# Delta-rule scan with two head groups in opposite row halves: 64x64 matmuls on alternating array quarters and a compact state

## The chip, the cores and the metric

The kernel runs on one core of a Trainium2 chip. The metric is the device time of one execution in microseconds. A core has a matmul engine (TensorE; PE in the profile, its weight loads PEld), a vector engine (VectorE; DVE), a scalar engine (ScalarE; ACT), a general engine (GpSimd; POOL) and a queue engine (SyncE; SP). Each runs its own instructions in their order and waits for the others by semaphores. TensorE multiplies a stationary operand (`lhsT`) by a moving one (`rhs`) and writes to PSUM, which has banks of 128 partitions by 512 float32.

## The reference

A decoder block with two token mixers on 1024 tokens of width 1024. Mixer A is a dilated window attention. Mixer B, which the change concerns, is a gated delta rule with 8 heads of 64 by 64, evaluated in 16 chunks of 64 tokens, one after the other:

```python
def step(state, inp):
    q_e, at, u_c, w_c, k_d, dec = inp
    v_new = u_c - jnp.einsum('bhck,bhkv->bhcv', w_c, state)
    o = jnp.einsum('bhck,bhkv->bhcv', q_e, state) + jnp.einsum('bhij,bhjv->bhiv', at, v_new)
    state = state * dec[..., None, None] + jnp.einsum('bhck,bhcv->bhkv', k_d, v_new)
    return state, o
```

Before the scan come projections, a causal convolution, norms and a triangular solve in each chunk; after it an RMS norm over each head's 64 outputs, a gate, an up-projection of both mixers, a sigmoid-gated merge, an output projection, a residual add and a last norm.

## The kernel before

All large products are float16 matmuls of a high and a low part: three matmuls of 128x512 for each eighth of the contraction (lines 150 to 152, helper `mm3_steps`). An object `Feed` holds the projections as units of 32 steps; a step (one tick) is those three matmuls. Code that has to wait for other engines calls `feed.tick(n)`, which puts n ticks of this filler on TensorE between its own matmuls. TensorE's order is thus the order in which the code is written; the other engines' instructions are ordered by the framework's scheduler, where `tc.high_priority()` moves some ahead.

The scan (lines 1164 to 1215) runs over 8 tiles `t` of 128 tokens and in each over two chunks `c2`, which lie in partitions 0 to 63 and 64 to 127. Everything of chunk `c2` lies in the row half `r`. In each chunk but the first:

- `pk` and `pq` (line 1180, PSUM tag S): four pairs of heads at a time, keys or queries (`kT`, `qT`: 128 partitions are two heads of 64) times the state `Sb`. `Sb` is 128 x 4 x 128: for each pair of heads a block-diagonal 128x128, half of it zeros, so that one matmul with contraction over 128 rows serves two heads. 8 matmuls with 128 moving columns.
- on VectorE `z = Rv - pk * bgk` (two operations on 64 partitions x 512), `oq = pq * eG`, `Sb *= dec`.
- `feed.tick(4)`, then `pvn` (line 1192, tag O): for each of 8 heads the solved triangle `U` times `z`, 64x64 matmuls, all in one row half and one column half of the array.
- `vn = pvn * rk`, `feed.tick(2)`, then `pS` (line 1200, tag G): 8 matmuls `kdec` times `vn` that read one row half and write the two column halves in turn; two additions into the diagonal blocks of `Sb`; `feed.tick(2)`.

After the two chunks of a tile `po` (line 1211, tag G) multiplies the masked scores `at` by `vn`: 16 matmuls of 64x64, eight in one quarter of the array, then eight in another. `ob = oq + po`, its square (ScalarE) and its sum follow. `PACE = (4, 2, 2)` holds the three tick counts. S and G have two banks each, O has one.

After the scan, `fac` is formed, `ob` is scaled for each tile (8 operations), `feed.tick(OB_LAG)` puts 12 ticks in between, and 8 groups of four 128x128 transposes (line 1231) bring `ob` into the layout of the gate `zs`, with two ticks between groups.

Ahead of the scan the step sizes `beta` and log decays `gg` are made from a small projection (lines 822 to 838), and one PSUM bank `pg` takes four small products (lines 845 to 855): the running sum of `gg` by `upto`, what is left by `later`, and the sums over a chunk.

A float32 matmul stands as one row in an order list and as two MATMUL instructions (two passes) in the trace; a float16 matmul and a transpose stand as one in both.

Of the kernel before, what the change touches and what calls it, by code (L numbers as in the profile page):

```python
# [56 lines left out]
def hybrid_block(ctx: ExitStack, tc: tile.TileContext, A):  # L57
# [718 lines left out]
    def conv_unit(hb, what, dst_of, then=None):  # L776

        def gen(w):
            for c in range(2):
                cidx = 4 * what + 2 * hb + c  # L780
                dst = dst_of(c)
                last = []
                for hf in range(2):
                    def take(p):
                        with tc.high_priority():
                            xc = pp_.tile([128, 515], F32, name="xc", tag="xc", bufs=2)
                            if hf == 0:
# [37 lines left out]
    beta = kp.tile([128, 8, 8], F32, name="beta")  # L825
    gg = kp.tile([128, 8, 8], F32, name="gg")
# [17 lines left out]
    ggf = gg.rearrange("p t h -> p (t h)")  # L844
    PE.matmul(pg[:, 0:64], lhsT=upto, rhs=ggf, start=True, stop=True, skip_group_check=True)
# [6 lines left out]
    for h2 in range(2):  # L852
        PE.matmul(pg[64 * h2:64 * h2 + 64, 128:192], lhsT=ones64,
                  rhs=gx.rearrange("p t c (q e) -> p (t c) q e", e=2)[:, :, :, h2],
                  start=False, stop=True, skip_group_check=True)
    SC.activation(eG.rearrange("p t h -> p (t h)"), pg[:, 0:64], AF.Exp)
# [18 lines left out]
    Sb = gp.tile([128, 4, 128], F32, name="Sb")  # L875
# [82 lines left out]
    def keys_side(hb):  # L958
# [202 lines left out]
    def pv(x):  # L1161
        return x.rearrange("p (h v) -> p h v", v=64)

    for t in range(8):
# [4 lines left out]
        oq = cp.tile([128, 8, 64], F32, name="oq", tag="oq", bufs=1)
        vn = cp.tile([128, 8, 64], F32, name="vn", tag="vn", bufs=2)  # L1170
        for c2 in range(2):
            ch = 2 * t + c2
            r = slice(64 * c2, 64 * c2 + 64)
            z = Rv[:, 0]
            if ch:
                z = cp.tile([128, 8, 64], F32, name="z", tag="z", bufs=1)
                pk, pq = [bank("S", 2), bank("S", 2)]
                for p, src in ((pk, kT), (pq, qT)):
                    for c in range(4):
                        PE.matmul(p[r, c * 128:c * 128 + 128], lhsT=src[c][:, ch], rhs=Sb[:, c],  # L1180
                                  start=(c == 0), stop=True, skip_group_check=True)
                with tc.high_priority():
                    TT(z[r], pv(pk[r]), bc(bgk[r, t], 64), ALU.mult)
                    TT(z[r], Rv[r, t], z[r], ALU.subtract)
                TT(oq[r], pv(pq[r]), bc(eG[r, t], 64), ALU.mult)
                TT(Sb, Sb, bc(dec[:, t, c2], 128), ALU.mult)
            else:
                GP.memset(oq[r], 0.0)
            feed.tick(PACE[0])
            pvn = bank("O", 1)  # L1190
            for h in range(8):
                PE.matmul(pvn[r, h * 64:h * 64 + 64], lhsT=U[h // 4][r, t, h % 2, (h % 4) // 2], rhs=z[r, h],  # L1192
                          start=(h == 0), stop=True, skip_group_check=True)
            with tc.high_priority():
                TT(vn[r], pv(pvn[r]), bc(rk[r, t], 64), ALU.mult)
            feed.tick(PACE[1])
            pS = bank("G", 2)
            for h in range(8):
                e = slice(64 * (h % 2), 64 * (h % 2) + 64)
                PE.matmul(pS[e, h // 2 * 64:h // 2 * 64 + 64], lhsT=kdec[r, h], rhs=vn[r, h],  # L1200
                          start=(h < 2), stop=True, skip_group_check=True)
            with tc.high_priority():
                for h2 in range(2):
                    e = slice(64 * h2, 64 * h2 + 64)
                    TT(Sb[e, :, e], Sb[e, :, e], pS[e, :256].rearrange("p (c v) -> p c v", v=64), ALU.add)
            feed.tick(PACE[2])
        po = bank("G", 2)
        for c2 in range(2):
            r = slice(64 * c2, 64 * c2 + 64)
            for h in range(8):  # L1210
                PE.matmul(po[r, h * 64:h * 64 + 64], lhsT=at[h // 4][r, t, h % 2, (h % 4) // 2], rhs=vn[r, h],  # L1211
                          start=(h == 0), stop=True, skip_group_check=True)
# [9 lines left out]
    TT(fac, fac, rq, ALU.mult)  # L1222
# [3 lines left out]
    for hf in range(2):  # L1226
        for ct in range(4):
            ts = slice(hf * 512, hf * 512 + 512)
            p = bank("G", 2)
            for t in range(4):  # L1230
                PE.transpose(p[:, t * 128:t * 128 + 128],
                             ob[:, 4 * hf + t, 2 * ct:2 * ct + 2].rearrange("p h v -> p (h v)"), ident)
            STT(zs[ct][:, ts], p, gnw, zs[ct][:, ts], ALU.mult, ALU.mult)
# [182 lines left out]
```

## Time and profile before

| | |
|---|---|
| time, three runs | 1176.77, 1179.36 (median), 1180.28 us |
| profiled execution | 1178.9 us, of which the span of the core is 1177.1 us |
| VectorE busy | 775.3 us (66%) |
| ScalarE busy | 490.6 us (42%) |
| DMA, mean | 98 GB/s |
| the scan, first `pvn` to first filler behind the last `po` | 804.3 to 959.5 us |

Times of instructions are in us from the start of the span. A row of the timeline has the start, the duration, the engine, the line, the operation, output and inputs, the size and how many instructions were merged into the row; in square brackets stands how long the engine was idle before, and what ended that. A busy time of TensorE is modelled: the matmuls are pipelined, so that from one row's start to the next row's start is the time that a burst took of the engine, and the printed duration is longer than that.

### The profile page before, as it was taken

What the parts mean: (1) busy time and instruction counts of PE and PEld (TensorE: products, weight loads), DVE (VectorE), ACT (ScalarE), POOL (GpSimd) and SP (SyncE); (2) the same over time, 40 slices, a digit from 0 to 9 for tenths busy, and PEclk for the clock granted to TensorE, in tenths of its full rate; (3) what the DMA queues carried; (4) which work ended last, traced back from release to release, by engine and by line L of the source; (5) the groups of instructions that cost most, each with busy time, mean ns of one, the idle gap of its engine ahead of it and who ended that gap; (6) DMA issues with size and microseconds to landing.
All of it is one profiled execution on the core that took longest, in us unless ns stands there. A gap on an engine that the chain in (4) does not pass through costs nothing.

```text
span 1177.1 us, 22738 instructions
## 1 busy us (share of the span) xinstructions
PE 1151.2 (98%) x9134; PEld 708.2 (60%) x9134; DVE 775.3 (66%) x1737; ACT 490.6 (42%) x1125; POOL 57.9 (5%) x103
## 2 busy tenths in 40 slices
PE   6999999999999999999999999999999999999997
PEld 6884765857758556756555444556666654444443
DVE  5776747568475489568859979846766663675233
ACT  6445746566465455456545233333221123331211
POOL 2110000000000000000000000000000000100000
PEclk9999999999999999999999999999999999999999
DMA  7154333423434323523114341421110116440232
GB/s 265 62 143 122 110 100 91 127 81 83 140 91 113 97 76 99 151 91 96 41 54 125 96 135 55 99 73 63 46 32 33 46 45 258 159 165 1 72 108 72
DMA packets 73050, 115.24 MB, mean 98 GB/s; under 512 B 30560, under 2 KB 41184, under 8 KB 72816
## 3 DMA queue, kind: packets, MB, share of 16 engines
q1 hardware_dynamic: 56064, 65.14, 19.0%
q0 software_dynamic: 12128, 44.11, 11.8%
q10 hardware_dynamic: 4752, 4.52, 1.1%
q8 instruction: 72, 1.18, 0.4%
q14 instruction: 34, 0.28, 0.1%
HBM read 73.70 MB, written 21.17 MB: 81 GB/s over the span
## 4 chain that ended last, share of the span: by engine, by line
PE 75%; DVE 12%; DMA 4%; SPq 3%; ACT 3%; issue 2%; ACTq 0%; DVEq 0%
PE ps_mm L150 19%; PE ps_mm L151 18%; PE ps_mm L152 18%; SPq L466 3%; PE ps_S L1180 2%; PE ps_G L607 2%; PE ps_O L1192 1%; DVE wlo L62 1%; PE ps_G L950 1%; PE ps_G L1211 1%; DVE rt L65 1%; PE ps_S L152 1%; PE ps_S L150 1%; PE ps_S L151 1%; DVE tl L65 1%
## 5 line engine op out<-in xcount | busy, mean ns | idle before, releaser
L150 PE MATMUL ps_mm<-h_hi,whi 128*128 128x512 f16 (+1 forms) x912 | 345.0, 378 | 0.1
L151 PE MATMUL ps_mm<-h_lo,whi 128*128 128x512 f16 (+1 forms) x912 | 343.9, 377 | 1.0 <-DVE h_lo L65 1.0
L152 PE MATMUL ps_mm<-h_hi,wlo 128*128 128x512 f16 (+1 forms) x912 | 343.9, 377 | 0.0
L152 PEld LDWEIGHTS <-wlo 128*128 128x128 f16 x1088 | 106.4, 98 | 122.8 <-issue 1.2
L150 PEld LDWEIGHTS <-whi 128*128 128x128 f16 x1088 | 106.2, 98 | 87.3 <-issue 2.6
L151 PEld LDWEIGHTS <-whi 128*128 128x128 f16 x1088 | 106.5, 98 | 79.8 <-issue 0.3
L597 ACT ACTIVATE sm<-sm,osb 128x128 f32<-128x128 f32 (+1 forms) x192 | 85.0, 443 | 93.2 <-DVE osb L593 92.6
L62 DVE SCALAR_TENSOR_TENSOR wlo<-wstage,whi 128x1024 f16<-128x1024 f32 x80 | 97.2, 1222 | 37.7 <-ACT whi L136 37.4
L150 PE MATMUL ps_mm<-whi,h_hi 128*128 128x256 f16 x384 | 105.1, 274 | 0.0
L151 PE MATMUL ps_mm<-wlo,h_hi 128*128 128x256 f16 x384 | 104.7, 273 | 0.1
L152 PE MATMUL ps_mm<-whi,h_lo 128*128 128x256 f16 x384 | 104.7, 273 | 0.0
L136 ACT ACTIVATE whi<-wstage 128x1024 f16<-128x1024 f32 x79 | 82.6, 1054 | 44.7 <-PE ps_mm L151 40.5
L593 DVE CUSTOM_DVE_ANT_0 sm<-ps_S,amask 128x128 f32<-128x128 f32 (+1 forms) x192 | 59.5, 348 | 30.8 <-PE ps_S L586 30.6
L65 DVE TENSOR_TENSOR tl<-ps_G,th 128x256 f16<-128x256 f32 (+1 forms) x96 | 52.2, 544 | 39.2 <-ACT th L612 38.8
L132 POOL DMA_DIRECT2D wstage<-in_w x68 | 35.9, 528 | 809.2 <-DVE wlo L62 615.2
L65 DVE TENSOR_TENSOR rt<-rx,tabs 128x512 f32<-128x512 f32 x96 | 65.0, 688 | 15.3 <-ACT rx L439 14.3
L62 DVE SCALAR_TENSOR_TENSOR ca<-xc,cw,ca 128x512 f32<-128x512 f32 x72 | 53.8, 747 | 2.2 <-ACT ca L793 1.6
L150 PE MATMUL ps_mm<-wo_hi,m_hi 128*128 128x512 f16 (+2 forms) x136 | 49.5, 366 | 0.0
L151 PE MATMUL ps_mm<-wo_lo,m_hi 128*128 128x512 f16 (+2 forms) x136 | 49.5, 366 | 0.0
L152 PE MATMUL ps_mm<-wo_hi,m_lo 128*128 128x512 f16 (+2 forms) x136 | 49.4, 366 | 0.0
L607 PE MATMUL ps_G<-cons,sm 128*128 128x128 f32 x280 | 46.4, 273 | 2.0 <-DVE tl L65 2.0
L151 PEld LDWEIGHTS <-h_hi 128*128 128x128 f16 x384 | 45.8, 119 | 1.3
(264 smaller groups left out, 1928.9 us busy)
## 6 DMA issues: line engine op xcount, KB each, us to landing
wstage<-in_w POOLq DMA_DIRECT2D x68, 512.0 KB, 4.6
og<-osb ACTq DMA_DIRECT2D x32, 132.0 KB, 2.1
og<-og SPq DMA_DIRECT2D x32, 132.0 KB, 2.2
gspa<-gst SPq DMA_DIRECT2D x16, 256.0 KB, 2.0
wstage<-in_w_up POOLq DMA_DIRECT2D x8, 512.0 KB, 4.7
sga<-gspa SPq DMA_DIRECT2D x8, 512.0 KB, 5.0
wstage<-in_w_out POOLq DMA_DIRECT2D x8, 512.0 KB, 4.2
xr<-in_x SPq DMA_DIRECT2D x8, 512.0 KB, 4.2
```

Of the source, the lines that this page charges most:

```text
L62: (eng or V).scalar_tensor_tensor(out, in0, scalar, in1, op0=op0, op1=op1)
L65: (eng or V).tensor_tensor(out, in0, in1, op)
L132: (eng or nc.gpsimd).dma_start(out=st, in_=src[:, 4 * c:4 * c + 4])
L136: SC.activation(hi[:, 4 * c:4 * c + 4], st, AF.Copy, scale=W_SCALE)
L150: PE.matmul(out, lhsT=wh(k), rhs=mh(k), start=first and i == 0, stop=False, skip_group_check=True)
L151: PE.matmul(out, lhsT=wh(k), rhs=ml(k), start=False, stop=False, skip_group_check=True)
L152: PE.matmul(out, lhsT=wl(k), rhs=mh(k), start=False, stop=last and i == len(ks) - 1, skip_group_check=True)
L466: nc.sync.dma_start(out=o, in_=pt[name][32 * hd:32 * hd + 32])
L593: V.tensor_tensor_reduce(P[:, u, :128 * nk], psc[:, u * 256:u * 256 + 128 * nk], mask, -cexp, -NEG, ALU.add, ALU.min, accum_out=osb[:, 256 ...
L597: SC.activation(P[:, u, :128 * nk], P[:, u, :128 * nk], AF.Exp, bias=osb[:, 256 + hd:257 + hd], scale=-1.0, accum_out=osb[:, 260 + hd:261 ...
L607: PE.transpose(pt[:, c:c + 128], P[:, u, i * 128:i * 128 + 128], ident)
L1180: PE.matmul(p[r, c * 128:c * 128 + 128], lhsT=src[c][:, ch], rhs=Sb[:, c], start=(c == 0), stop=True, skip_group_check=True)
```

## The change

Heads 0 to 3 (`hb = 0`) stay as they were. For heads 4 to 7 (`hb = 1`) the two chunks of every tile swap their row halves. A chunk's eight heads then fill both row halves: four heads in one, four in the other, side by side in 256 columns in place of 512.

- The state becomes compact: `Sb` is 128 x 4 x 64, without the zero blocks. `pk` and `pq` become 16 matmuls of 64x64 for each head alone, which go through the four quarters in turn and share two banks (`pkq`), one for each row half that is read.
- `pvn` and `po` alternate between heads of the two groups, so that neighbouring matmuls lie in opposite quarters. `pS` writes two banks, one for each group.
- VectorE's operations of the scan work on 128 partitions: `vn` and `Sb *= dec` on 256 elements, `z`'s product and `oq` in two parts of 128, the subtraction in two parts of 64 partitions x 256, the additions into `Sb` in two parts of 128.
- What is multiplied along with them is laid out again: `by_chunk` copies `eG`, `rk`, `bgk` and `rq` into `eGs`, `rks`, `bgks`, `rqs`. The convolution's last operation writes heads 4 to 7 in two parts with the chunks swapped. For `beta` and `gg` two matmuls with a shifted identity swap the halves of heads 4 to 7, and ScalarE copies the result back (line 872 after the change) ahead of the products with `upto` and `later`.
- The first chunk's `z` is copied from `Rv` by ScalarE.
- The transposes behind the scan are 8 of 64 rows for each group in place of 4 of 128, into two banks, and the gate's multiplication is two operations.

```diff
+    hi4 = bg[:, :, :, 4:8]
+    for b in range(2):
+        PE.matmul(pg[64 * b:64 * b + 64, 192:256], lhsT=ident[:, 64 - 64 * b:128 - 64 * b], rhs=hi4,
                   start=False, stop=True, skip_group_check=True)
+    SC.copy(hi4, pg[:, 192:256].rearrange("p (a t h) -> p a t h", a=2, t=8))
+    PE.matmul(pg[:, 0:64], lhsT=upto, rhs=ggf, start=False, stop=True, skip_group_check=True)
+    PE.matmul(pg[:, 64:128], lhsT=later, rhs=ggf, start=False, stop=True, skip_group_check=True)
     SC.activation(eG.rearrange("p t h -> p (t h)"), pg[:, 0:64], AF.Exp)
+    by_chunk(eGs, eG)
...
-    Sb = gp.tile([128, 4, 128], F32, name="Sb")
+    Sb = gp.tile([128, 4, 64], F32, name="Sb")
...
+    order = [(hb, j) for j in range(4) for hb in range(2)]
...
-                pk, pq = [bank("S", 2), bank("S", 2)]
-                for p, src in ((pk, kT), (pq, qT)):
-                    for c in range(4):
-                        PE.matmul(p[r, c * 128:c * 128 + 128], lhsT=src[c][:, ch], rhs=Sb[:, c],
-                                  start=(c == 0), stop=True, skip_group_check=True)
+                pkq = [bank("S", 2), bank("S", 2)]
+                for i, src in enumerate((kT, qT)):
+                    for j in range(2):
+                        for n, (e, hb) in enumerate(((0, 0), (1, 1), (0, 1), (1, 0))):
+                            b, c, o = c2 ^ hb, 2 * hb + j, (2 * i + j) * 64
+                            PE.matmul(pkq[e][rows(b), o:o + 64], lhsT=src[c][rows(e), 2 * t + b], rhs=Sb[rows(e), c],
+                                      start=(i == 0 and j == 0), stop=True, skip_group_check=True)
                 with tc.high_priority():
-                    TT(z[r], pv(pk[r]), bc(bgk[r, t], 64), ALU.mult)
-                    TT(z[r], Rv[r, t], z[r], ALU.subtract)
-                TT(oq[r], pv(pq[r]), bc(eG[r, t], 64), ALU.mult)
-                TT(Sb, Sb, bc(dec[:, t, c2], 128), ALU.mult)
+                    for e in range(2):
+                        TT(z[:, e::2], hv(pkq[e][:, :128]), bc(bv[:, e::2], 64), ALU.mult)
+                    for hb in range(2):
+                        r = rows(c2 ^ hb)
+                        TT(z[r], Rv[r, t, 4 * hb:4 * hb + 4], z[r], ALU.subtract)
+                for e in range(2):
+                    TT(ov[:, e::2], hv(pkq[e][:, 128:256]), bc(ev[:, e::2], 64), ALU.mult)
+                TT(Sb, Sb, bc(dec[:, t, c2], 64), ALU.mult)
...
             pvn = bank("O", 1)
-            for h in range(8):
-                PE.matmul(pvn[r, h * 64:h * 64 + 64], lhsT=U[h // 4][r, t, h % 2, (h % 4) // 2], rhs=z[r, h],
-                          start=(h == 0), stop=True, skip_group_check=True)
+            for n, (hb, j) in enumerate(order):
+                r = rows(c2 ^ hb)
+                PE.matmul(pvn[r, j * 64:j * 64 + 64], lhsT=U[hb][r, t, j % 2, j // 2], rhs=z[r, j],
+                          start=(n < 2), stop=True, skip_group_check=True)
...
-            pS = bank("G", 2)
+            pS = [bank("G", 2), bank("G", 2)]
+            for q in range(2):
+                for hb, e in ((0, 0), (1, 1), (0, 1), (1, 0)):
+                    r, c = rows(c2 ^ hb), 2 * hb + q
+                    PE.matmul(pS[hb][rows(e), q * 64:q * 64 + 64], lhsT=kdec[r, 2 * c + e], rhs=vn[r, c2, 2 * q + e],
+                              start=(q == 0), stop=True, skip_group_check=True)
...
         po = bank("G", 2)
         for c2 in range(2):
-            r = slice(64 * c2, 64 * c2 + 64)
-            for h in range(8):
-                PE.matmul(po[r, h * 64:h * 64 + 64], lhsT=at[h // 4][r, t, h % 2, (h % 4) // 2], rhs=vn[r, h],
-                          start=(h == 0), stop=True, skip_group_check=True)
+            for n, (hb, j) in enumerate(order):
+                r, o = rows(c2 ^ hb), (4 * c2 + j) * 64
+                PE.matmul(po[r, o:o + 64], lhsT=at[hb][r, t, j % 2, j // 2], rhs=vn[r, c2, j],
+                          start=(c2 == 0 and n < 2), stop=True, skip_group_check=True)
...
-            p = bank("G", 2)
+            ps2 = [bank("G", 2), bank("S", 2)]
+            hb, h0 = ct // 2, ct % 2 * 2
             for t in range(4):
-                PE.transpose(p[:, t * 128:t * 128 + 128],
-                             ob[:, 4 * hf + t, 2 * ct:2 * ct + 2].rearrange("p h v -> p (h v)"), ident)
-            STT(zs[ct][:, ts], p, gnw, zs[ct][:, ts], ALU.mult, ALU.mult)
+                for b in range(2):
+                    c2 = b ^ hb
+                    PE.transpose(ps2[b][:, 64 * t:64 * t + 64],
+                                 ob[rows(b), 4 * hf + t, 4 * c2 + h0:4 * c2 + h0 + 2].rearrange("p h v -> p (h v)"),
+                                 ident[rows(b), rows(b)])
```

How instructions stand now, at the places that the prediction speaks of. On TensorE, the products with the state in the second chunk of the scan (`ps_S` is the bank, `Sb` the state, `kT` and `qT` with a buffer number are the pairs of heads). Before:

```order
L1180 MATMUL ps_S<-Sb,kT_740 64x128
L1180 MATMUL ps_S<-Sb,kT_741 64x128
L1180 MATMUL ps_S<-Sb,kT_742 64x128
L1180 MATMUL ps_S<-Sb,kT_743 64x128
L1180 MATMUL ps_S<-Sb,qT_8020 64x128
L1180 MATMUL ps_S<-Sb,qT_8021 64x128
L1180 MATMUL ps_S<-Sb,qT_8022 64x128
L1180 MATMUL ps_S<-Sb,qT_8023 64x128
```

On TensorE, the same place after the change:

```order
L1212 MATMUL ps_S<-Sb,kT_740 64x64
L1212 MATMUL ps_S<-Sb,kT_742 64x64 x2
L1212 MATMUL ps_S<-Sb,kT_740 64x64
L1212 MATMUL ps_S<-Sb,kT_741 64x64
L1212 MATMUL ps_S<-Sb,kT_743 64x64 x2
L1212 MATMUL ps_S<-Sb,kT_741 64x64
L1212 MATMUL ps_S<-Sb,qT_8027 64x64
L1212 MATMUL ps_S<-Sb,qT_8029 64x64 x2
L1212 MATMUL ps_S<-Sb,qT_8027 64x64
L1212 MATMUL ps_S<-Sb,qT_8028 64x64
L1212 MATMUL ps_S<-Sb,qT_8030 64x64 x2
L1212 MATMUL ps_S<-Sb,qT_8028 64x64
```

Eight products of 64x128 became sixteen of 64x64, with heads of the two groups in turn.

On VectorE, the fifth chunk's start, where a weight split (`wlo`) and the gate's work (`zs`) stand ahead of the scan's own `z`. Before:

```order
L65 TENSOR_TENSOR Sb<-Sb,ps_G 64x4x64 x2
L62 SCALAR_TENSOR_TENSOR wlo<-wstage,whi 128x1024
L62 SCALAR_TENSOR_TENSOR zs<-zt,ps_mm 128x512
L65 TENSOR_TENSOR z<-ps_S,bgk 64x512
L62 SCALAR_TENSOR_TENSOR zs<-zs,oTa_5297 128x512
L65 TENSOR_TENSOR z<-Rv,z 64x512
L65 TENSOR_TENSOR Rv<-oq,ps_G 128x512
L65 TENSOR_TENSOR osa_10654<-zs,osa_10654 128x512
```

On VectorE, the same place after the change:

```order
L65 TENSOR_TENSOR Sb<-Sb,ps_G 128x128 x2
L62 SCALAR_TENSOR_TENSOR wlo<-wstage,whi 128x1024
L62 SCALAR_TENSOR_TENSOR zs<-zt,ps_mm 128x512
L65 TENSOR_TENSOR z<-ps_S,bgks 128x2x64 x2
L62 SCALAR_TENSOR_TENSOR zs<-zs,oTa_5297 128x512
L65 TENSOR_TENSOR z<-Rv,z 64x256 x2
L65 TENSOR_TENSOR Rv<-oq,ps_G 128x512
L65 TENSOR_TENSOR osa_10716<-zs,osa_10716 128x512
L65 TENSOR_TENSOR vn<-ps_O,rks 128x256
```

The scan's operations are smaller and more, and the filler's operations stand among them at the same places; `vn` now comes ahead of the sum over `oq` and of `Sb *= dec`.

On TensorE, the small products ahead of the scan (`gx`, `bg` are what is multiplied, `cons` holds the constant matrices), after the change:

```order
L152 MATMUL ps_mm<-h_hi,wlo 128x512
L864 MATMUL ps_G<-gx,ones_6948 64x64 x2
L870 MATMUL ps_G<-bg,cons 64x64 x2
L874 MATMUL ps_G<-bg,cons 128x64
L875 MATMUL ps_G<-bg,cons 128x64
L150 LDWEIGHTS whi
```

Before, the two 128x64 products (lines 845 and 846) stood first and read `gg` directly; now they stand behind the swap on L870 and ScalarE's copy, with no filler in between.

More of the change, by code (lines that the diff above doesn't have):

```diff
@@ L806, in conv_unit, with by_chunk @@
         feed.add(("gdn", hb, what), A["w"][gdn_unit(hb, what)], gen)
+    def by_chunk(dst, x, hbs=(0, 1)):
+        for hb in hbs:
+            for b in range(2):
+                r = slice(64 * b, 64 * b + 64)
+                V.tensor_copy(dst[r, :, b ^ hb], x[r, :, 4 * hb:4 * hb + 4])
     gate_unit(1, gate_spill)
@@ L824, in hybrid_block @@
     STT(ba, pv[:, :, 0:16], P_SCALE, ba, ALU.mult, ALU.add)
-    beta = kp.tile([128, 8, 8], F32, name="beta")
-    gg = kp.tile([128, 8, 8], F32, name="gg")
+    bg = kp.tile([128, 2, 8, 8], F32, name="bg")
+    beta, gg = bg[:, 0], bg[:, 1]
     tmpa = pp_.tile([128, 8, 8], F32, name="tmpa")
@@ L839, in hybrid_block @@
     eG = kp.tile([128, 8, 8], F32, name="eG")
+    eGs = kp.tile([128, 8, 2, 4], F32, name="eGs")
     eGl = kp.tile([128, 8, 8], F32, name="eGl")
@@ L854, in hybrid_block @@
                   rhs=gx.rearrange("p t c (q e) -> p (t c) q e", e=2)[:, :, :, h2],
+                  start=True, stop=True, skip_group_check=True)
+    hi4 = bg[:, :, :, 4:8]
+    for b in range(2):
+        PE.matmul(pg[64 * b:64 * b + 64, 192:256], lhsT=ident[:, 64 - 64 * b:128 - 64 * b], rhs=hi4,
                   start=False, stop=True, skip_group_check=True)
+    SC.copy(hi4, pg[:, 192:256].rearrange("p (a t h) -> p a t h", a=2, t=8))
+    ggf = gg.rearrange("p t h -> p (t h)")
+    PE.matmul(pg[:, 0:64], lhsT=upto, rhs=ggf, start=False, stop=True, skip_group_check=True)
+    PE.matmul(pg[:, 64:128], lhsT=later, rhs=ggf, start=False, stop=True, skip_group_check=True)
     SC.activation(eG.rearrange("p t h -> p (t h)"), pg[:, 0:64], AF.Exp)
+    by_chunk(eGs, eG)
     SC.activation(eGl.rearrange("p t h -> p (t h)"), pg[:, 64:128], AF.Exp)
@@ L882, in hybrid_block @@
     bgk = gp.tile([128, 8, 8], F32, name="bgk")
+    rks = gp.tile([128, 8, 2, 4], F32, name="rks")
+    rqs = gp.tile([128, 8, 2, 4], F32, name="rqs")
+    bgks = gp.tile([128, 8, 2, 4], F32, name="bgks")
     def rnorm(dst, ssum, post):
@@ L963, in keys_side @@
         TT(bgk[:, :, hsl], brk[:, :, hsl], eG[:, :, hsl], ALU.mult)
+        by_chunk(bgks, bgk, (hb,))
+        by_chunk(rks, rk, (hb,))
         pack = p2_.tile([128, 2, 8, 4], F32, name="pack", tag="pack", bufs=1)
@@ L1159, in hybrid_block, with hv, rows @@
     ob = Rv
-    def pv(x):
+    def hv(x):
         return x.rearrange("p (h v) -> p h v", v=64)
+    def rows(b):
+        return slice(64 * b, 64 * b + 64)
+    order = [(hb, j) for j in range(4) for hb in range(2)]
     for t in range(8):
@@ L1194, in hybrid_block @@
             with tc.high_priority():
-                TT(vn[r], pv(pvn[r]), bc(rk[r, t], 64), ALU.mult)
+                TT(vn[:, c2], hv(pvn[:, :256]), bc(rks[:, t, c2], 64), ALU.mult)
             feed.tick(PACE[1])
-            pS = bank("G", 2)
-            for h in range(8):
-                e = slice(64 * (h % 2), 64 * (h % 2) + 64)
-                PE.matmul(pS[e, h // 2 * 64:h // 2 * 64 + 64], lhsT=kdec[r, h], rhs=vn[r, h],
-                          start=(h < 2), stop=True, skip_group_check=True)
+            pS = [bank("G", 2), bank("G", 2)]
@@ L1202, in hybrid_block @@
+            for q in range(2):
[3 more added lines that the diff above has]
+                              start=(q == 0), stop=True, skip_group_check=True)
             with tc.high_priority():
-                for h2 in range(2):
-                    e = slice(64 * h2, 64 * h2 + 64)
-                    TT(Sb[e, :, e], Sb[e, :, e], pS[e, :256].rearrange("p (c v) -> p c v", v=64), ALU.add)
+                for hb in range(2):
+                    sv = Sb[:, 2 * hb:2 * hb + 2]
+                    TT(sv, sv, hv(pS[hb][:, :128]), ALU.add)
@@ L1221, in hybrid_block @@
     V.reciprocal(fac, fac)
-    TT(fac, fac, rq, ALU.mult)
+    TT(fac, fac, rqf, ALU.mult)
     for t in range(8):
```

40 lines of the change are left out of this document (25 added, 15 removed).

## The prediction

> **What bounds the kernel now.** I read the page first (busy shares, then the chain of work that ended last), then the busy time by stretches for the scan alone, then the timeline of one chunk in it.
>
> ```profile
> span 1177.1 us, 22738 instructions
> PE 1151.2 (98%) x9134; PEld 708.2 (60%) x9134; DVE 775.3 (66%) x1737; ACT 490.6 (42%) x1125; POOL 57.9 (5%) x103
> PE 75%; DVE 12%; DMA 4%; SPq 3%; ACT 3%; issue 2%; ACTq 0%; DVEq 0%
> ```
>
> TensorE is busy 98% of the span and holds 75% of the chain. An average proves nothing for the scan, so the stretch from its first to its last product comes next (columns: the stretch, its length, then busy time and instructions of PE, PEld, DVE, ACT, POOL, then the granted clock, the DMA share and GB/s).
>
> ```profile
> 804.28:959.48 155.20, 155.20 (x1382) 97.19 (x1381) 102.25 (x164) 28.70 (x42) 3.75 (x8) 1.00 0.12 38
> ```
>
> In 155.2 us TensorE has no gap that this view shows, at full clock; VectorE is at 102.25 / 155.20 = 66%. Busy is modelled, so the timeline has to confirm it:
>
> ```profile
> 826.42 0.38 PE L152 MATMUL ps_mm<-h_hi,wlo 128*128 128x512 f16 x1
> 826.73 0.68 PE L1200 MATMUL ps_G<-vn,kdec 64*64 64x64 f32 x16
> 827.34 0.39 PE L150 MATMUL ps_mm<-h_hi,whi 128*128 128x512 f16 x1
> ...
> 828.74 1.09 PE L1180 MATMUL ps_S<-Sb,kT 128*64 128x128 f32 x8
> ...
> 829.66 1.04 PE L1180 MATMUL ps_S<-Sb,qT 128*64 128x128 f32 x8
> 829.86 0.69 DVE L65 TENSOR_TENSOR z<-ps_S,bgk 64x512 f32<-64x512 f32 x1 [1.56 <-PE ps_S L1180]
> ...
> 830.63 0.39 PE L150 MATMUL ps_mm<-h_hi,whi 128*128 128x512 f16 x1
> ...
> 833.33 1.14 PE L1192 MATMUL ps_O<-z,MT 64*64 64x64 f32 x16
> 834.40 0.39 PE L150 MATMUL ps_mm<-h_hi,whi 128*128 128x512 f16 x1
> 834.50 0.69 DVE L65 TENSOR_TENSOR vn<-ps_O,rk 64x512 f32<-64x512 f32 x1 [1.06 <-PE ps_O L1192]
> ...
> 835.80 0.68 PE L1200 MATMUL ps_G<-vn,kdec 64*64 64x64 f32 x16
> ```
>
> Every burst follows the filler with the same step, 0.31 us from 826.42 to 826.73. VectorE waits for TensorE (`vn` 1.06 us), not the other way: `vn` ends at 834.50 + 0.69 = 835.19 and is needed at 835.80. So what the small matmuls take from one row's start to the next comes straight off the span: `pk` and `pq` 830.63 - 828.74 = 1.89, `pvn` 834.40 - 833.33 = 1.07, `pS` 827.34 - 826.73 = 0.61.
>
> **The bursts, one by one.** `pvn` and `pS` have eight 64x64 products each (16 instructions). `pvn`, always in one quarter, takes 1.07; `pS`, whose neighbours write different column halves, 0.61. I read this as neighbours in different quarters overlapping. The other rows:
>
> ```profile
> 837.81 1.90 PE L1211 MATMUL ps_G<-vn,E 64*64 64x64 f32 x32
> 839.64 0.54 PE L1180 MATMUL ps_S<-Sb,kT 128*64 128x128 f32 x3
> ...
> 619.17 1.15 PE L950 MATMUL ps_G<-kT 64*64 64x64 f32 x32
> 620.26 0.39 PE L150 MATMUL ps_mm<-h_hi,whi 128*128 128x512 f16 x1
> ...
> 782.12 0.44 PE L1027 MATMUL ps_S<-T1p,MT 32*32 32x32 f32 x16
> 782.49 0.39 PE L150 MATMUL ps_mm<-h_hi,whi 128*128 128x512 f16 x1
> ```
>
> `po` takes 1.83 for sixteen products. L950, sixteen 64x64 products with the column halves in turn, takes 1.09. Sixteen at 1.09 and eight at 0.61 make 0.48 for eight more, or 0.06 for one product, and 0.13 for a burst's entry and exit. In L1027 (32x32) neighbours differ in row half and column half and write one bank: sixteen instructions in 0.37. If its products were serial like `pvn`'s, with half the columns, they would take (1.07 - 0.13) / 2 + 0.13 = 0.60. So row halves overlap as well. What the trace does not have is a neighbour in the same columns and the other rows, which the new `pkq` and `pS` have at every second step. Bounds: such a step is free, as above, or serial, which costs (1.07 - 0.61) / 8 = 0.06 for each. I take free, because both kinds of half that the trace shows are.
>
> - `pkq`, sixteen products, 1.09 in place of 1.89: 0.80 x 15 chunks = 12.0.
> - `pvn` at 0.61 in place of 1.07: 0.46 x 16 = 7.4.
> - `po` at 1.09 in place of 1.83: 0.74 x 8 = 5.9.
> - `pS`: still eight products with neighbours in turn, 0.
> - Behind `po` the next `pkq` follows at once, now in the same 64x64 shape: one entry and exit less, 0.13 x 7 = 0.9.
>
> Together **26.2 us less**.
>
> **What comes back.** VectorE's sizes, by rows that group all of a kind in the scan and in the merge before it:
>
> ```profile
> L65 DVE TENSOR_TENSOR Sb<-Sb,ps_G 64x256 f32<-64x256 f32 x32 | 13.4, 418 | 12.9 <-PE ps_G L1200 12.4
> L65 DVE TENSOR_TENSOR z<-ps_S,bgk 64x512 f32<-64x512 f32 x15 | 10.3, 688 | 10.2 <-PE ps_S L1180 10.0
> ...
> L65 DVE TENSOR_TENSOR Y<-ps_S,brk 32x128 f32<-32x128 f32 x32 | 9.3, 290 | 8.7 <-PE ps_S L1027 8.0
> ```
>
> 512 elements take 0.69, 256 take 0.42, 128 take 0.29; a count of partitions does not show (rows of 64 and 128 partitions agree). `z` stays near 1.4 (2 x 0.29 + 2 x 0.42 for 2 x 0.69), `vn` falls to 0.42, the additions from 2 x 0.42 to 2 x 0.29. A chunk's scan work on VectorE falls from 3 x 0.69 + 0.69 + 0.69 + 0.84 = 4.3 to 4 x 0.29 + 2 x 0.42 + 0.42 + 0.42 + 0.58 = 3.4. So nothing on the path grows, and a chunk's ticks (0.22 x 24 matmuls) still cover it. The cover is thin where filler work stands ahead, as in the fifth chunk:
>
> ```profile
> 838.79 1.22 DVE L62 SCALAR_TENSOR_TENSOR wlo<-wstage,whi 128x1024 f16<-128x1024 f32 x1 [1.31 <-ACT whi L136]
> 840.05 0.69 DVE L62 SCALAR_TENSOR_TENSOR zs<-zt,ps_mm 128x512 f32<-128x512 f32 x1
> ```
>
> `wlo` comes from the filler's pace and keeps its distance to the start of `po` (837.81), so `zs` ends at 840.74 as before. Behind it stand two products (0.58), another `zs` (0.69) and two subtractions (0.84): 842.85. TensorE, with `po` and `pkq` in 1.09 + 0.96 and 12 filler matmuls in 833.33 - 830.63 = 2.70, is there at 842.56, against 844.2 before. Queued behind the waiting `pvn` is the filler itself, so the 0.3 is lost. The eight `wlo` of the scan come in pairs, so this comes four times: I take **1.0** for waits of the scan, between 0 and 8 (below).
>
> Ahead of the scan the swap adds a round trip:
>
> ```profile
> 501.09 0.42 DVE L849 TENSOR_SCALAR gx<-gg,cons 128x64 f32<-128x64 f32 x2
> ...
> 501.20 0.41 PE L845 MATMUL ps_G<-gg,cons 128*128 128x64 f32 x2
> ...
> 501.76 0.33 PE L853 MATMUL ps_G<-gx,ones 128*64 128x64 f32 x4
> ...
> 502.03 0.39 PE L150 MATMUL ps_mm<-h_hi,whi 128*128 128x512 f16 x1
> ...
> 502.14 0.22 ACT L856 ACTIVATE eG<-ps_G 128x64 f32<-128x64 f32 x1 [0.30 <-PE ps_G L853]
> ```
>
> TensorE now waits for `gx` (done at 501.51), does eight instructions of L853's kind (to about 502.2), ScalarE copies in 0.22, and L845's and L846's kind takes 501.76 - 501.20 = 0.56 behind it: filler at about 503.2 in place of 502.03, **1.15 more**, since nothing is put in between. ScalarE's table load, now behind the copy, delays only `eG`.
>
> The solve of the triangles is the next cover:
>
> ```profile
> 699.73 0.43 PE L1044 MATMUL ps_O<-MT,Y 32*32 32x32 f32 x14 [0.51 <-DMA MT<-u_d]
> ...
> 651.32 0.18 DVE L966 COPY pack<-rk 128x32 f32<-128x32 f32 x1
> 651.41 0.18 DVE L65 TENSOR_TENSOR stmp<-As,X 128x31 f32<-128x31 f32 x1
> ```
>
> TensorE already waits 0.51 for the solved blocks there, so VectorE's additions before it are not hidden: four small copies at 0.10 (the step from 651.32 to 651.41) and about three convolution outputs in two parts (2 x 0.42 - 0.69 = 0.15 each) make 0.85. A later wait for `Rv` may swallow part; I take **0.6**, between 0 and 1.5.
>
> Behind the scan:
>
> ```profile
> 957.65 1.90 PE L1211 MATMUL ps_G<-vn,E 64*64 64x64 f32 x32
> ...
> 964.42 4.90 DVE L65 TENSOR_TENSOR Rv<-Rv,fac 128x512 f32<-128x512 f32 x8
> ...
> 967.26 0.60 PE L1231 MATMUL ps_G<-cons,Rv 128*128 128x128 f32 x4
> 967.70 0.38 PE L150 MATMUL ps_mm<-h_hi,whi 128*128 128x512 f16 x1
> ```
>
> The first transposes need four of the eight scalings, at 964.42 + 4 x 0.61 = 966.9, a time that hangs on `wlo` and the gate and not on `po`. TensorE comes there 0.74 earlier, at 966.5: **0.4** lost. The eight groups of transposes take 967.70 - 967.26 = 0.44 each; 8 half-height ones in a new shape cost 0.13 more for entry and exit, and between 0.22 (neighbours overlap, half the columns) and 0.88 (8 x 0.11, no overlap) themselves. I take the lower end with some loss, **0.5** for all eight groups, with ends at -0.7 and 4.6.
>
> Sum: -26.2 + 1.0 + 1.15 + 0.6 + 0.4 + 0.5 = -22.6. From the profiled execution's 1178.9 (its span is 1177.1) that is **1156.3**; the median of the three runs is 0.5 above that execution.
>
> **Rivals.**
> - *Rows do not overlap in one bank.* `pvn` and `po` write one bank from both row halves; without overlap their 7.4 + 5.9 stay: 1156.3 + 13.3 = 1169.6. L1027 speaks against it, in another tile size. The Trainium skill, TensorEngine Tiling, section Restrictions and Gotchas, states such a rule: different row tiles cannot access the same PSUM bank at once; by it the sum would be -9.3, and L1027's 0.37 against a serial 0.60 does not bear it out.
> - *Same columns, other rows are serial.* Eight steps of `pkq` and four of `pS` in a chunk at 0.06: 0.06 x (8 x 15 + 4 x 16) = 11: 1167.3. If this and the case above hold together, row halves never overlap, and the change does nothing: 1156.3 + 13.3 + 11 = 1180.6.
> - *VectorE's queue becomes the wait.* If two filler operations stand ahead of `vn` in every chunk, it ends 1.38 + 0.42 + 0.1 = 1.9 behind `pvn`, where 835.80 - 834.40 = 1.4 are covered: 16 x 0.5 = 8: 1164.3. For it: VectorE would be at about 90 of 129 us, 70%. Against it: in the order `vn` stands behind at most two such operations, which start before `pvn` ends.
> - *Four quarters overlap deeper than two.* `pkq` and `pS` visit four, so 0.06 could become 0.03: 0.03 x (16 x 15 + 8 x 16) = 11 more: 1145.3. Against it: each product is two instructions in the same quarter in order, so only the second of one and the first of the next can lie side by side. The Trainium skill, TensorEngine Tiling, section Tiling Modes, has tiles work independently, which would allow it; no run here shows four.
> - *Slower: a change of row half stalls the array.* The four kinds of burst have 16 x 15 + 8 x 16 + 8 x 16 + 16 x 8 = 624 products. Today they take 15 x 1.89 + 16 x 1.07 + 16 x 0.61 + 8 x 1.83 = 69.9. With 48 x 0.13 = 6.2 for entries and exits and 3.6 of the losses above, the change is lost at (69.9 - 6.2 - 3.6) / 624 = 0.096 for each. If each switch of row half cost the 0.09 that a change of shape costs on entry (0.31 less a filler step of 0.22), a product would take 2 x 0.06 + 0.09 = 0.21: 94 us more than at 0.06, 1250. L1027 speaks against it.
>
> **How the numbers follow.** Forecast (1152 to 1161) 0.58; waits of VectorE 0.13; same-column steps serial 0.10; one-bank rows serial 0.07; deeper overlap 0.05; slower 0.04; row halves never overlapping 0.03. The range 1151 to 1167 takes in the forecast, nearly all of the VectorE case and about half of the two serial ones (parts of them cost less): 0.8. A measurement of this kernel can tell about 0.3%, 3.5 us, from no change: faster 0.93, same 0.03, slower 0.04.
>
> **What would show it.** `pkq` at 1.1 from its first row to what follows, `pvn` 0.6, `po` 1.1, `pS` 0.6; first `pvn` to the end of the last `po` some 130 us in place of 155. A `pS` above 0.61 shows the same-column step serial; a `pvn` near 1.07 the bank rule; steps above 0.31 ahead of `pvn`, `pS` or `pkq`, with VectorE named, the queue. About 1.1 more between the `gx` products and the next filler, and a longer wait for `u_d` in the merge, are the losses outside. The prediction is wrong if the bursts do not shrink, or if TensorE shows waits of several us in the scan.

## The result, and the profile after

| | before | after |
|---|---|---|
| time, median of four runs each | 1178.2 us (1176.77 to 1180.28) | 1147.85 us (1144.65 to 1149.21) |
| ratio, 95% interval | | 0.974 (0.971 to 0.976) |
| profiled execution, its span | 1178.9, 1177.1 us | 1144.65, 1142.9 us |
| first `pvn` to first filler behind the last `po` | 155.2 us | 120.9 us |

The change makes the kernel faster, by 30.4 us between the medians and 34.3 us between the profiled executions. The forecast was 1156.3; the time lies 3 us below the low end of its range and 2.5 us above the rival in which four quarters overlap deeper than two (1145.3).

The page of the changed kernel (span; busy time and share of each engine; shares of the chain that ended last), then the stretch of the scan in the view by stretches:

```profile
span 1142.9 us, 23354 instructions
PE 1116.6 (98%) x9410; PEld 672.3 (59%) x9410; DVE 757.9 (66%) x1818; ACT 491.7 (43%) x1128; POOL 57.5 (5%) x103
PE 74%; DVE 18%; DMA 3%; ACT 2%; issue 2%; SPq 1%; DVEq 0%; ACTq 0%
803.87:924.76 120.89, 120.24 (x1621) 63.64 (x1621) 81.07 (x213) 28.05 (x42) 3.86 (x8) 1.00 0.16 50
```

The shares of the engines look as they did: TensorE 98%, VectorE 66%. That is why shares alone could not say what the change was worth. The scan holds the same filler (372 matmuls in both traces, at the same full clock) and is 34.3 us shorter; VectorE in it is at 81.07 / 120.89 = 67%. TensorE's rows of the timeline, for one chunk and for the scan's end:

```profile
821.45 0.46 PE L1241 MATMUL ps_G<-vn,kdec 64*64 64x64 f32 x16
821.84 0.39 PE L150 MATMUL ps_mm<-h_hi,whi 128*128 128x512 f16 x1
...
823.24 0.46 PE L1212 MATMUL ps_S<-Sb,kT 64*64 64x64 f32 x16
...
823.52 0.41 PE L1212 MATMUL ps_S<-Sb,qT 64*64 64x64 f32 x16
...
823.87 0.39 PE L150 MATMUL ps_mm<-h_hi,whi 128*128 128x512 f16 x1
...
826.57 0.79 PE L1232 MATMUL ps_O<-z,MT 64*64 64x64 f32 x16
827.29 0.39 PE L150 MATMUL ps_mm<-h_hi,whi 128*128 128x512 f16 x1
...
919.88 0.68 PE L1232 MATMUL ps_O<-z,MT 64*64 64x64 f32 x16
920.49 0.39 PE L150 MATMUL ps_mm<-h_hi,whi 128*128 128x512 f16 x1
...
923.68 1.15 PE L1252 MATMUL ps_G<-vn,E 64*64 64x64 f32 x32
924.76 0.39 PE L150 MATMUL ps_mm<-h_hi,whi 128*128 128x512 f16 x1
```

From one row's start to the next, `pS` (L1241) takes 0.39 where 0.61 was forecast, and `pkq` (L1212, 32 instructions) 0.63 where 1.09 was forecast. `po` (L1252) takes 1.08 and an undisturbed `pvn` (L1232, at 919.88) 0.61, both as forecast. So the two bursts that visit all four quarters are far shorter than those that visit two, for the same number of instructions: `pS` 0.39 against `pvn` 0.61 with 16 each, `pkq` 0.63 against `po` 1.08 with 32 each.

The `pvn` at 826.57 takes 0.72, not 0.61. The reason is in VectorE's timeline:

```profile
826.21 0.42 DVE L65 TENSOR_TENSOR z<-Rv,z 64x256 f32<-64x256 f32 x1
```

The second half of `z` is ready at 826.21 + 0.42 = 826.63, after the burst has begun with the first half. The wait is inside the burst, where no gap between rows shows it.

### The profile page after: what moved, and what is told of

Its sections match the earlier page's. It is cut to its first block, busy times and chain, and to the rows that moved or that the text cites. A ratio compares the mean times of both kernels' runs of the same rounds, so it can differ in the third digit from the quotient of the medians.

```text
span 1142.9 us, 23354 instructions
## 1 busy us (share of the span) xinstructions
PE 1116.6 (98%) x9410; PEld 672.3 (59%) x9410; DVE 757.9 (66%) x1818; ACT 491.7 (43%) x1128; POOL 57.5 (5%) x103
## 4 chain that ended last, share of the span: by engine, by line
PE 74%; DVE 18%; DMA 3%; ACT 2%; issue 2%; SPq 1%; DVEq 0%; ACTq 0%
PE ps_mm L150 20%; PE ps_mm L151 19%; PE ps_mm L152 19%; DVE wlo L62 2%; PE ps_G L607 2%; DVE ca L62 2%; DVE X L65 2%; DVE stmp L65 2%; PE ps_S L151 1%; PE ps_S L150 1%; PE ps_S L152 1%; DVE rt L65 1%; PE ps_S L586 1%; PE ps_S L584 1%; DMA og<-og 1%
```

## The experiments

The question was what sets the time of a burst. On the rule of the prediction, only neighbours overlap: 0.06 us for a product whatever the number of quarters. The reading formed from the trace of the changed kernel is that **each quarter works through its own instructions**, one in 0.058 us (`pvn` before, 16 in one quarter, 1.07; `pS` before, 8 in each of two, 0.61: 0.46 / 8), with 0.15 for entry and exit of the burst (1.07 - 16 x 0.058). Then the fullest quarter sets the time. The expectations call it Q, and Q3 in a sharper form that came of four of the runs (the first two below and the two on the kernel before); B is its rival. Each group of runs has its own times of the kernel before, from the same chip: 1178.54 us (seven runs) for those four, 1179.2 us (nine runs) for the others.

### The order of the quarters, first form

In the changed kernel `pkq` and `pS` go first through one pair of opposite quarters, then through the other pair. The products are the same. (The edits of this and the next two runs are written here as plain loops.)

```diff
-                for i, src in enumerate((kT, qT)):
-                    for j in range(2):
-                        for n, (e, hb) in enumerate(((0, 0), (1, 1), (0, 1), (1, 0))):
+                for two in (((0, 0), (1, 1)), ((0, 1), (1, 0))):
+                    for i, src in enumerate((kT, qT)):
+                        for j in range(2):
+                            for e, hb in two:
```

> The changed kernel, with the products of pkq and pS in another order: first all that lie in the two diagonal quarters, then all in the two others; same instructions, same banks. Theory Q (each quarter of the array takes its instructions by itself, so a burst lasts 0.058 us x the instructions of the quarter that has most, plus 0.15, if the order offers all quarters in turn): only two quarters side by side at a time, pkq 0.63 -> 1.08 us, pS 0.39 -> 0.61, the kernel 0.45 x 15 + 0.22 x 16 = 10 us slower than the changed one, which is what the prediction had forecast for it. Rival B (the separate banks and the smaller products give the time, not the order): pkq and pS unchanged, 0 us.

Measured 1148.61 us (1148.28 to 1151.67), 0.9751 of before (0.9734 to 0.9768). The burst takes 0.91 at the median, and `pS` 0.41. TensorE's timeline of one `pkq`:

```profile
827.80 0.45 PE L1210 MATMUL ps_S<-Sb,kT 64*64 64x64 f32 x8
828.09 0.22 PE L1210 MATMUL ps_S<-Sb,qT 64*64 64x64 f32 x2
828.10 0.27 PE L1210 MATMUL ps_S<-Sb,kT 64*64 64x64 f32 x2
...
828.71 0.39 PE L150 MATMUL ps_mm<-h_hi,whi 128*128 128x512 f16 x1
```

The order matters, so B, for which the burst would stay at 0.63, falls. But 0.91 is also less than the 1.08 of Q, and the rows show why. The code has eight instructions on `kT` in the first pair, then eight on `qT` in it, then those on `kT` in the second pair. The latter begin at 828.10, when only two of the eight on `qT` have begun: six, three in each of the two quarters, are still waiting. So the engine reaches past instructions that wait for a busy quarter, up to **three for each quarter**. With that, of the eight steps of the first pair five go by before the second pair joins in with its eight: 13 x 0.058 + 0.15 = 0.90.

The expected 10 us did not come: 1148.61 stands against the changed kernel's 1147.85 in the table above, and the ranges overlap. In the trace the scan is 2.8 us longer (123.7 against 120.9), since `pkq` costs only 0.28 more and `pvn` loses most of its waits (0.63 in the mean, against 0.74). So it is the burst that speaks against B, not the kernel's time.

### Two products of a quarter in a row

```diff
-                    for j in range(2):
-                        for n, (e, hb) in enumerate(((0, 0), (1, 1), (0, 1), (1, 0))):
+                    for e, hb in ((0, 0), (1, 1), (0, 1), (1, 0)):
+                        for j in range(2):
```

`pS` likewise. A run is now four instructions in one quarter: one that runs and three that wait.

> The changed kernel, with two products of the same quarter (four instructions) behind each other before the next quarter comes, in pkq and pS. Theory Q with an engine that looks past a waiting instruction to those of other quarters: pkq stays near 0.63, pS near 0.39. Rival I (strict order: an instruction never starts ahead of the one before it): each run of four costs three steps of 0.054, pkq 8 x 0.16 + 0.15 = 1.45 us, pS 4 x 0.16 + 0.15 = 0.8, the kernel 0.8 x 15 + 0.4 x 16 = 19 us slower than the changed one.

Measured 1145.92 us (one run, so the trace has to carry this one). In TensorE's timeline:

```profile
823.76 0.48 PE L1210 MATMUL ps_S<-Sb,kT 64*64 64x64 f32 x16
824.04 0.47 PE L1210 MATMUL ps_S<-Sb,qT 64*64 64x64 f32 x16
824.45 0.39 PE L150 MATMUL ps_mm<-h_hi,whi 128*128 128x512 f16 x1
```

`pkq` takes 0.69, `pS` 0.41: nearly nothing is lost (0.63 and 0.39), though at every second step neighbouring products now lie in the same quarter. The prediction's reading, that only neighbours overlap, cannot give this.

### Four products of a quarter in a row

All four products of a quarter, eight instructions, stand in a row in `pkq`; `pS` stays as in the run before.

```diff
-                for i, src in enumerate((kT, qT)):
-                    for j in range(2):
-                        for n, (e, hb) in enumerate(((0, 0), (1, 1), (0, 1), (1, 0))):
+                for e, hb in ((0, 0), (1, 1), (0, 1), (1, 0)):
+                    for i, src in enumerate((kT, qT)):
+                        for j in range(2):
```

> The changed kernel, with all four products of a quarter (eight instructions) behind each other in pkq, quarter after quarter. Theory Q3 (each quarter takes its instructions by itself at 0.058 us each, and the engine puts up to three more behind the one that runs; a fourth holds up everything behind it): each quarter starts 8 - 4 = 4 to 5 steps after the one before, pkq (8 + 3 x 4.5) x 0.058 + 0.15 = 1.4 us in place of 0.63, the kernel about 0.75 x 15 = 11 us slower than the changed one. Rival E (the engine looks past any number of waiting instructions): 0.63, 0 us. Rival I (strict order): 32 x 0.056 + 0.1 = 1.9 us, 19 us slower.

Measured 1155.73 us (1154.5 to 1158.41), 0.9801 of before (0.9775 to 0.9826). On the same chip the changed kernel itself, run again, took 1144.93 (1144.14 to 1150.64).

```profile
826.08 0.44 PE L1210 MATMUL ps_S<-Sb,kT 64*64 64x64 f32 x4
826.36 0.22 PE L1210 MATMUL ps_S<-Sb,qT 64*64 64x64 f32 x1
826.37 0.27 PE L1210 MATMUL ps_S<-Sb,kT 64*64 64x64 f32 x1
...
827.55 0.39 PE L150 MATMUL ps_mm<-h_hi,whi 128*128 128x512 f16 x1
```

The burst takes 1.47 and the time rises by 10.8 us, with the same 32 instructions on the same operands in four quarters. (The bursts cost 15 x 0.84 = 12.6 more; 2.0 come back, because `pvn` no longer waits inside and takes 0.61 in all 16 chunks.) Once a run is longer than one running and three waiting instructions, the fifth holds up everything behind it. Each quarter but the last has five of its eight steps alone: (5 + 5 + 5 + 8) x 0.058 + 0.15 = 1.48. This bounds the waiting places from above, as the run before does from below. The rows show it directly: the second quarter begins, with its `kT` at 826.37, when five of the first quarter's eight have begun and three still wait. In the first experiment six waited at that moment, three in each of two quarters, so the limit is one for each quarter and not one on all that wait.

### The kernel before, `po` with the row halves in turn

The kernel before with two loops exchanged, nothing else of the change:

```diff
-        for c2 in range(2):
-            r = slice(64 * c2, 64 * c2 + 64)
-            for h in range(8):
+        for h in range(8):
+            for c2 in range(2):
+                r = slice(64 * c2, 64 * c2 + 64)
```

> The kernel before, with one thing changed: po's loops over heads and chunks are swapped, so that its sixteen products alternate between two opposite quarters in place of eight and eight. Theory Q: 32 instructions, 16 in each of two quarters, 16 x 0.058 + 0.15 = 1.08 us in place of 1.83, 6 us faster than before (1172 against 1178). Rival B (opposite quarters in one bank do not overlap, the gain comes from two banks): 1.83, no change.

Measured 1172.41 us (1171.32 to 1172.61), 0.9945 of before (0.9930 to 0.9960).

```profile
835.98 1.15 PE L1211 MATMUL ps_G<-vn,E 64*64 64x64 f32 x32
837.06 0.32 PE L1180 MATMUL ps_S<-Sb,kT 128*64 128x128 f32 x1
```

`po` takes 1.08 in place of 1.83, and 8 x 0.75 = 6.0 stands against 6.1 between the medians. The two row halves write different partitions of one bank. The rival in which rows do not overlap in one bank is refuted by this, and by `pvn` at 0.61. The Trainium skill, TensorEngine Tiling, section Restrictions and Gotchas, has the rule; here it does not hold.

### The kernel before, `pk` and `pq` by head

The other part of the change that can stand alone: 64x64 products for each head, whose neighbours write the same columns from the two row halves, into two banks.

```diff
-                for p, src in ((pk, kT), (pq, qT)):
+                for i, src in enumerate((kT, qT)):
                     for c in range(4):
-                        PE.matmul(p[r, c * 128:c * 128 + 128], lhsT=src[c][:, ch], rhs=Sb[:, c],
-                                  start=(c == 0), stop=True, skip_group_check=True)
+                        for e in range(2):
+                            f, o = slice(64 * e, 64 * e + 64), (4 * i + c) * 64
+                            PE.matmul(pkq[e][r, o:o + 64], lhsT=src[c][f, ch], rhs=Sb[f, c, f],
+                                      start=(i == 0 and c == 0), stop=True, skip_group_check=True)
```

> The kernel before, with its layout, but pk and pq as sixteen products of 64x64 for each head alone; neighbours lie in the same columns and the two row halves in turn, in two banks; VectorE's z product and oq become two operations of 64x256 each. Theory Q: 16 instructions in each of two quarters, 1.08 us in place of 1.89, 0.8 x 15 = 12 us faster than before (1166 against 1178). Rival C (same columns, other rows are serial): 32 x 0.054 + 0.15 = 1.9, no change, or some us slower for VectorE's additional operations.

Measured 1168.15 us (1167.41 to 1169.68), 0.9909 of before (0.9892 to 0.9925). In TensorE's timeline, and what TensorE waited for (the sum, how often, the longest):

```profile
828.24 0.68 PE L1182 MATMUL ps_S<-Sb,kT 64*64 64x64 f32 x16
828.76 0.63 PE L1182 MATMUL ps_S<-Sb,qT 64*64 64x64 f32 x16
829.33 0.39 PE L150 MATMUL ps_mm<-h_hi,whi 128*128 128x512 f16 x1
```

```profile
PE ps_O L1196 <- DVE z L65: 2.8, 7, 0.7
```

The burst takes 1.09 in place of 1.89, the value that two quarters give (16 x 0.058 + 0.15 = 1.08). The step that the prediction could not see in any row, same columns and other rows, is as free as the others. The bursts save 13.4 us in the trace: 0.81 where `pkq` stands alone, 1.13 in the seven places where it follows `po` (2.59 for both in place of 3.72), less two bursts that wait 0.5 inside. Of this 2.8 come back as waits for `z`, whose product on VectorE is now two operations, and 0.8 as waits for `vn` and `Sb`. The scan is 9.9 us shorter (145.3 against 155.2); 10.4 lie between the medians.

### `pvn` one group after the other

In the changed kernel the four heads of one group come first, then those of the other: eight instructions of a quarter in a row.

```diff
-            for n, (hb, j) in enumerate(order):
+            for hb, j in [(hb, j) for hb in range(2) for j in range(4)]:
```

> The changed kernel, with pvn's four products of the first head group ahead of the four of the second (eight instructions in one quarter, then eight in the opposite one). Theory Q3: the second quarter starts 4 to 5 steps late, pvn (8 + 4.5) x 0.058 + 0.15 = 0.87 us in place of 0.61 without waits, 4 us slower in all. Rival E: 0.61. Rival I: 1.07, as before the change.

Measured 1148.4 us (one run).

```profile
820.63 0.96 PE L1232 MATMUL ps_O<-z,MT 64*64 64x64 f32 x16
821.53 0.39 PE L150 MATMUL ps_mm<-h_hi,whi 128*128 128x512 f16 x1
```

0.90 in place of 0.61, between the 1.07 of one quarter and the 0.61 of a strict alternation, and what the count gives: (5 + 8) x 0.058 + 0.15 = 0.90. The scan grows from 120.9 to 123.6 us, and not by the expected 4 us, since the changed kernel's `pvn` already loses 2.0 us to waits inside.

### The changed kernel again, and the waits that it left

Two runs ask how much the small losses are worth: the changed kernel unchanged, and one with five ticks ahead of `pvn` in place of four (one less behind the additions to `Sb`), one more tick ahead of the `gx` products, and one between ScalarE's copy and the products with `upto` and `later`; two ticks less later on keep the filler's count.

```diff
-PACE = (4, 2, 2)
+PACE = (5, 2, 1)
...
-    feed.tick(5)
+    feed.tick(6)
...
     SC.copy(hi4, pg[:, 192:256].rearrange("p (a t h) -> p a t h", a=2, t=8))
+    feed.tick(1)
...
-    feed.tick(ATT_LEAD)
+    feed.tick(ATT_LEAD - 2)
```

> The changed kernel once more, for comparison on the same chip: all theories say 1148 us within 0.4%.

> The changed kernel with the waits that it shows covered: PACE (5, 2, 1) in place of (4, 2, 2), which moves one tick of each chunk from behind pS to ahead of pvn, and in the small products ahead of the scan one tick more before them and one between ScalarE's copy and what reads it (two fewer after). If the waits are as the trace reads: pvn 0.74 -> 0.62 in the mean (2 us in all), the wait of 0.5 us for vn in one chunk stays or goes, about 1 us ahead of the scan: 3 us faster than the changed kernel. Rival: the additions into Sb end too late for pkq with one tick, 16 x 0.1 to 0.3 us lost: same or up to 3 us slower.

Measured 1144.93 us (1144.14 to 1150.64, five runs; 0.9722 of before, 0.9698 to 0.9747) and 1145.88 us (1144.91 to 1147.11; 0.9716, 0.9697 to 0.9736). They cannot be told apart, so the expected 3 us did not come. By stages: `pvn` falls to 0.61 in all 16 chunks, from 0.74 in the mean (16 x 0.13 = 2.0 us). But the missing tick uncovers the state, as TensorE's waits in this kernel show (in the changed kernel there is none for `Sb`, and 0.4 for `vn`):

```profile
PE ps_S L1213 <- DVE Sb L65: 1.0, 2, 0.5
PE ps_G L1242 <- DVE vn L65: 0.7, 3, 0.3
```

Without the three filler matmuls that now stand ahead of the first `pvn`, the scan is as long as it was (120.3 us and 3 x 0.22 against 120.9). Ahead of the scan something was saved: from the last filler matmul before the `gx` products to the first `pvn` it takes 303.9 us, where the changed kernel takes 305.5 in its first profile and 304.8 in that of its repetition, with the same number of filler matmuls. These 0.9 to 1.6 us drown in what the stretch before varies by: the last filler matmul there starts at 498.40 us in the first profile of the changed kernel and at 503.15 us in that of its repetition.

## Why the prediction missed

**The step that failed** is one sentence of the rival "Four quarters overlap deeper than two": "Against it: each product is two instructions in the same quarter in order, so only the second of one and the first of the next can lie side by side." It gave the right mechanism a chance of 0.05. In the sum it left only neighbours to overlap: a product of `pkq` at 0.06 us whatever the number of quarters (burst 1.09, measured 0.63) and the gain of `pS` at 0 (burst 0.61, measured 0.39). The range was cut off above that rival. The trace of before already had the row against it. TensorE's timeline in a window that ends 0.05 us after a burst's first instruction, for `pS` and for `pvn` of the kernel before and for `pkq` of the changed one:

```profile
826.73 0.27 PE L1200 MATMUL ps_G<-vn,kdec 64*64 64x64 f32 x2
```

```profile
833.33 0.27 PE L1192 MATMUL ps_O<-z,MT 64*64 64x64 f32 x1
```

```profile
823.24 0.29 PE L1212 MATMUL ps_S<-Sb,kT 64*64 64x64 f32 x4
```

One, two and four instructions begin at once: as many as the burst has quarters. If only the second instruction of a product could lie beside the first of the next, `pS` too would begin with one. The merged rows of 16 instructions, on which the prediction rested, cannot show this. What is more, in the change of burst behind `po`, where the code has all of `po` first:

```profile
831.36 0.27 PE L1212 MATMUL ps_S<-Sb,kT 64*64 64x64 f32 x2
831.40 0.23 PE L1252 MATMUL ps_G<-vn,E 64*64 64x64 f32 x2
```

Two instructions of `pkq`, in quarters that `po` does not use, start ahead of the last two of `po`. The count of quarters gives the joined burst as well: 16 instructions of `po` and 8 of `pkq` in each of the two fullest, 24 x 0.058 + 0.15 = 1.54, where the trace has 1.55 (forecast 1.09 + 0.96 = 2.05).

Point by point, in the terms of the sum (means over the bursts of the changed kernel's trace; 8 of the 15 `pkq` stand alone, 7 join a `po`):

| term | forecast | measured |
|---|---|---|
| `pkq`, 1.89 to 0.63 or 0.65 | 12.0 | 15 x 1.25 = 18.8 |
| `pS`, 0.61 to 0.39 | 0 | 16 x 0.22 = 3.5 |
| `pvn`, 1.07 to 0.61 | 7.4 | 7.4, less the waits inside |
| `po`, 1.83 to 1.08 | 5.9 | 6.0 |
| `po` and `pkq` joined | 0.9 | 7 x 0.16 = 1.1 |
| waits of the scan | -1.0 | -2.0, inside `pvn` (mean 0.74) |
| **the scan** | **25.2** | **34.8 by these terms, 34.3 by the rows** |

- The scan is 9.1 us shorter than forecast, and `pkq` (6.8 more) with `pS` (3.5) make up all of it. Everything else in the scan holds to about 1 us.
- **The swap ahead of the scan** was right in place and near in size. The row before the change, then those after it:

```profile
500.85 0.38 PE L152 MATMUL ps_mm<-h_hi,wlo 128*128 128x512 f16 x1
```

```profile
498.40 0.38 PE L152 MATMUL ps_mm<-h_hi,wlo 128*128 128x512 f16 x1
499.69 0.34 PE L864 MATMUL ps_G<-gx,ones 128*64 128x64 f32 x4 [0.92 <-issue]
499.83 0.31 PE L870 MATMUL ps_G<-bg,cons 128*64 128x64 f32 x4
500.44 0.43 PE L874 MATMUL ps_G<-bg,cons 128*128 128x64 f32 x2 [0.30 <-ACT bg L872]
500.72 0.39 PE L875 MATMUL ps_G<-bg,cons 128*128 128x64 f32 x2
500.94 0.38 PE L150 MATMUL ps_mm<-h_hi,whi 128*128 128x512 f16 x1
```

  From the last filler to the next it takes 500.94 - 498.40 = 2.54, before 502.03 - 500.85 = 1.18: 1.36 more, against 1.15. Most of it stands ahead of L864, which now comes first and has to wait; only 0.30 is the wait for ScalarE's copy. The repetition of the changed kernel takes 2.02 there, 0.84 more, because it waits 0.4 and not 0.9 ahead of L864. The forecast of 1.15 lies between the two, but its parts do not add up to it: 502.2 + 0.22 + 0.56 is 502.98, which is 0.95 more and not 1.15.
- **The solve and the merge.** The wait for `u_d` did not grow (0.4, before 0.5); of the two waits for `Rv` the later grew and the earlier shrank. Before the change, then after it (L1044 and L1068 have become L1070 and L1094):

```profile
PE ps_O L1044 <- DVE Rv L65: 1.0, 1, 1.0
PE ps_O L1068 <- DVE Rv L65: 0.9, 1, 0.9
```

```profile
PE ps_O L1094 <- DVE Rv L65: 1.8, 1, 1.8
PE ps_O L1070 <- DVE Rv L65: 0.5, 1, 0.5
PE ps_O L1070 <- DMA MT<-u_d: 0.4, 1, 0.4
```

  The stretch between the small products and the scan is 0.7 longer, against 0.6: the size right, the place named wrong. The three waits together grew by 0.3 (2.4 to 2.7); where the rest arises is not shown, so that the size may be luck.
- **Behind the scan**: from the first filler behind `po` to the one behind the last transposes 20.9 us, before 20.3; 0.6 more, against 0.4 + 0.5. The transposes cost what was forecast (13.0 from the first to the filler behind the last, before 12.6); the wait of 0.4 ahead of them did not come (7.9 to the first of them, before 7.8).
- **The sum by stages**: -34.3 + 1.4 + 0.7 + 0.6 = -31.6, against -22.6. The profiled executions differ by 34.3 because the stretch up to the small products happens to be 2.4 shorter in the second (its last filler starts at 498.40 and not at 500.85; over the traces of all runs that start lies between 498.40 and 503.15, and those of the three kernels without the change lie among the others); the medians differ by 30.4 in one group of runs and 34.3 in the other, on both sides of the sum.
- **The rivals.** One bank and same columns were free, as taken: the runs on `po` and on `pk` by head show it, apart from the rest of the change. VectorE's queue cost 2.0 us, twice the 1.0 of the sum and a quarter of the rival's 8. A change of row half does not stall. The case that came had a chance of 0.05; its 1145.3 lies among the executions measured (1144.65 to 1149.21, and 1144.93 at the median of the second group). The Trainium skill, TensorEngine Tiling, section Tiling Modes, states that tiles work independently: by that rule `pkq` and `pS` shrink once more, and the runs agree.

## What to carry to other kernels

For bursts of small matmuls count the instructions of each array quarter, not of the burst: if the quarters are offered in turn, the fullest quarter times the step (0.058 us here) and 0.15 for entry and exit give the time. They reproduce `pvn` and `pS` of the kernel before too, and with the three waiting places also its `po`, which takes one quarter after the other: 13 steps go by before the second quarter's 16 begin, (13 + 16) x 0.058 + 0.15 = 1.83. So spread the products over all four quarters and offer them in turn; a run of four instructions in one quarter costs almost nothing, runs of eight more than double the burst (0.63 to 1.47). All this was measured with 64x64 float32 products of 64 columns alone. Before a rival is given a small chance for a reason of order, look at the starts of single instructions in a narrow window, since a merged row cannot bear that reason out.

## What the runs showed of the hardware that was not expected

- A quarter takes one float32 instruction of 64x64 in 0.058 us, independently of the other quarters; up to three wait for a quarter without holding up the others. With 4 instructions in the fullest quarter a burst takes 0.39 (`pS`), with 8 it takes 0.61 to 0.63 (`pvn`, `pkq`), with 16 it takes 1.08 (`po`). What sets the 0.058 stays open: each instruction comes with its own weight load, and no run separates the two.
- Matmul instructions do not start in the order of the code when their quarters differ (831.36 ahead of 831.40 above); the description of the kernel before, where each engine runs its instructions in the order of the code, has to be read with this exception for TensorE. The Trainium skill, TensorE: Matmul & The Clock Gate, section Part 3: Packing small matmuls, states that matmuls start and end strictly in order; this trace's starts differ from it, and the starts decide. Their ends are modelled, and no run shows those.
- Row halves that write different partitions of one bank overlap fully (`po` 1.08 against 1.83). Row halves that write the same partitions of one bank were not tried.
